# Four low parts, a row block of W_down, staging loads, two roots and a spread: moved or rewritten in a hybrid gMLP and Mamba-2 layer

## The chip, the core and the metric

The kernel runs on one core of a Trainium2 chip. TensorE multiplies matrices, VectorE (DVE), ScalarE (ACT) and GpSimd (POOL) work elementwise, and SyncE (SP) issues transfers. The metric is the device time of one launch in microseconds.

## What is computed

One layer on 1024 tokens of 1024 channels, everything in fp32:

```python
h   = RMSNorm_pre(x)
P   = h @ W_in                    # u, v (gMLP, 512 each), z (512), x, B, C (512, 256, 256), dt (8)
A   = u * (W_s layer_norm(gelu(v)) + b)          # within chunks of 128 tokens, causal
B   = rms(ssd(conv(x, B, C), dt) * silu(z))      # 8 heads of 64, 2 groups of 128 states
x   = x + RMSNorm_post(concat[A, B] @ W_out)
x   = x + RMSNorm_post2(relu(RMSNorm_pre2(x) @ W_up)^2 @ W_down)     # 4096 hidden
```

## The kernel before

A product in fp32 is made of three products of shorter numbers: each operand is split in a high part (a cast, names ending in h) and a low part (the number less its high part, names ending in l), and TensorE adds high by high, low by high and high by low. The splitting of the weights goes on beside the products all through the kernel. The high part is cast by ACT, and the low part is a subtraction, up to W_out on POOL and in W_down on VectorE.

The 1024 tokens are taken in two halves of 512. In a half the weights come in units of 512 KB: units 0 to 7 make B, C and x, 8 to 11 z, 12 to 15 v, 16 to 19 u, and 20 to 23 the first four blocks of W_out; the second half then uses the same units again. For each unit SP loads the weights into a staging buffer ws (there are two), ACT casts wh, the low part wl is subtracted from ws and wh, and where the unit comes again, `keep` stores wl to DRAM (wd). In the second half `again` loads ws once more for the cast and loads wl from wd. SP is one queue: a transfer that waits for its data or its buffer holds up those behind it.

The program's start is an order written by hand (PRO_OPS): for a token tile t, S sums squares on ACT, R makes the reciprocal root on VectorE (Newton steps on one column, each waiting for the last), N multiplies by the root and the norm weights wpre, T transposes on TensorE, H and L split the transposed tile hT. W and V are the cast and the low part of units 0 and 1, M and C a multiplication of tile 2 on POOL and ACT. PRO_LOADS is the order of the first loads: digits for token tiles, w for wpre, a and b for units 0 and 1. What follows, until the W_up products, is ordered by a scheduler that takes its estimates and the dependences; where an engine is `held`, it keeps the order in which the code is written. gg is the decay tile of the Mamba part, loaded by SP from the DRAM tile acd; carry is the last three columns of a block of x, B or C, kept for the convolution. The later token tiles are transposed into tx and split into hTh and hTl as the first.

The gate norm (second function below) makes a root for each token and spreads the four chunks' columns along 128 columns in the bank psgr, by a product with the identity.

W_down is a list `seq` of products, VectorE held. For product m the loop writes the load of piece m + 3, the splitting of piece m + 2 (`preps`), the products, and, at the last of a group, the emptying of the four PSUM banks into an accumulator (`flush`). The last four row blocks of W_down stand behind `seq` in the same lists; their low parts are wldl0 to wldl3, and their products go into the banks pl.

Of the kernel before, what the change touches and what calls it, by code (L numbers as in the profile page):

```python
# [13 lines left out]
ALU = mybir.AluOpType  # L14

P = 128
SEQ = 1024
D = 1024
# [28 lines left out]

PRO_LOADS = "0w1a23b"  # L50
PRO_BANK = (0, 0, 1, 2)
PRO_OPS = ("S0 R0 S1 W0 N0 R1 T0 H00 N1 V0 S2 H01 L00 S3 L01 T1 H10 L10 M2 H11 R23 W1 V1 L11 N3 C2 "
           "T2 T3 H20 H21 L21 H31 H30 L20 L30 L31 X")


# [1 line left out]
def hymba_kernel(ctx, tc, x, norm_mix_pre, w_in, gm_ln_w, gm_ln_b, gm_w_s, gm_b_s,  # L57
                 conv_w, conv_b, dt_bias, a_log, d_skip, ssm_norm_w, w_out,
                 norm_mix_post, norm_ffn_pre, w_up, w_down, norm_ffn_post, out):
    nc = tc.nc  # L60
# [51 lines left out]
    def f(ap):  # L112
        return ap.bitcast(F32)
# [93 lines left out]
    staged = {}  # L207
# [10 lines left out]
    def load_unit(eng=None):  # L218
        i = state["load"]
        if i >= len(units):  # L220
            return
        state["load"] += 1
        if id(units[i]) in first:
            again(i)
            return
        first[id(units[i])] = i
        if i not in staged:
            stage_unit(i)
        st, shape = staged.pop(i)
        wh = wpool.tile(shape, F32R, tag="wh", bufs=N_SPLIT, name=f"wh{i}")  # L230
        wl = wpool.tile(shape, F32R, tag="wl", bufs=N_SPLIT, name=f"wl{i}")
        split(wh, wl, st, eng)
        ready.append((wh, wl))
        keep(i)

    def keep(i):

# [4 lines left out]
    def again(i):  # L242
        if i not in staged:
            stage_unit(i)
        st, shape = staged.pop(i)
        wh, wl = [wpool.tile(shape, F32R, tag=t_, bufs=N_SPLIT, name=f"{t_}{i}") for t_ in ("wh", "wl")]
        nc.sync.dma_start(f(wl.rearrange("p a b -> p (a b)")), parts[first[id(units[i])]])
        act.copy(wh, st)
        ready.append((wh, wl))

# [116 lines left out]
    def step(op):  # L367
        kind, arg = op[0], op[1:]
        t = int(arg[0]) if arg else 0
        if kind == "S":  # L370
            ssx[t] = sumsq(x0[t], f"ssx0{t}")
        elif kind == "R":
            chains = [rstd_steps(ssx[int(c)], D) for c in arg]
            for c, steps in zip(arg, chains):
                rx[int(c)] = next(steps)
            while chains:
                chains = [c for c in chains if next(c, 0) is None]
        elif kind == "N":
            dve.scalar_tensor_tensor(x0[t], x0[t], rx[t], wpre, op0=ALU.mult, op1=ALU.mult)
        elif kind == "M":  # L380
            for q in range(2):
                qs = slice(q * 512, (q + 1) * 512)
                pool.tensor_tensor(x0[t][:, qs], x0[t][:, qs], wpre[:, qs], op=ALU.mult)
        elif kind == "C":
            act.activation(x0[t], x0[t], AF.Copy, scale=rx[t])
        elif kind == "T":
            for q in range(2):
                ps = (mm_bank, ss_bank, mi_bank)[PRO_BANK[t]](f"tx0{t}_{q}")
                psx[t, q] = ps.rearrange("p (k c) -> p k c", c=P)
                for k in range(4):  # L390
                    c0 = (4 * q + k) * P
                    pe.transpose(psx[t, q][:, k, :], x0[t][:, c0:c0 + P], ident)
        elif kind in "HL":
            q = int(arg[1])
            h, l = [y[:, 4 * q:4 * q + 4, t * P:(t + 1) * P] for y in hT]
            if kind == "H":
                act.copy(h, psx[t, q])
            else:
                dve.tensor_tensor(l, psx[t, q], f(h), op=ALU.subtract)
        elif kind == "W":  # L400
            st, shape = staged.pop(t)
            wh = wpool.tile(shape, F32R, tag="wh", bufs=N_SPLIT, name=f"wh{t}")
            wl = wpool.tile(shape, F32R, tag="wl", bufs=N_SPLIT, name=f"wl{t}")
            act.copy(wh, st)
            units01[t] = wh, wl, st
        elif kind == "V":
            wh, wl, st = units01[t]
            pool.tensor_tensor(wl, st, f(wh), op=ALU.subtract)
            ready.append((wh, wl))
            first[id(units[t])] = t  # L410
            keep(t)
            state["load"] += 1
        else:
            small_setup()
# [306 lines left out]
    def gate_norm(H, g):  # L721
        nm = f"{g}{H.tg}"
        if g == 0:
            H.mb = s8("mixbh" + H.tg, F32R), s8("mixbl" + H.tg, F32R)
        mh, ml = H.mb
        zs = H.zt[2 * g], H.zt[2 * g + 1]
        for i in range(2):
            y = H.xg[g][:, i, :]
            dve.tensor_mul(y, y, zs[i])
            act.activation(zs[i], y, AF.Square)  # L730
        dve.tensor_add(zs[0], zs[0], zs[1])
        ps = mi_bank("psgn" + nm)
        for c in range(NCH):
            pe.matmul(ps[:, c:c + 1], lhsT=zs[0][:, c * P:(c + 1) * P], rhs=ones[:, 0:1],
                      start=True, stop=True)
        rt = row_rstd(ps[:, 0:NCH], 256)
        r = mi_bank("psgr" + nm)
        for c in range(NCH):
            pe.matmul(r[:, c * P:(c + 1) * P], lhsT=rt[:, c:c + 1].broadcast_to([P, P]), rhs=ident,
                      start=True, stop=True)  # L740
        for i in range(2):
            b = 2 * g + i
            y = H.xg[g][:, i, :]
            dve.scalar_tensor_tensor(y, y, cols[:, 40 + b:41 + b], r, op0=ALU.mult, op1=ALU.mult)
            split(mh[:, b, :], ml[:, b, :], y)
            H.mix[4 + b] = (mh[:, b, :], ml[:, b, :])
# [484 lines left out]
    for m, (n, g, i) in enumerate(seq):  # L1231
        gs = SG[n]
        k = m - seq.index((n, gs[0], ORD[0]))
        if k == len(gs):
            w_load(n + 1, 0)
        elif k == 5 * len(gs) + 1:
            w_load(n + 1, 1)
        floads[m + 3]()
        preps[m + 2]()
        (fh, fl), (h, l) = pcs[g, i]  # L1240
        if g == gs[0]:
            banks[i] = banks[MORE[i]] if i in MORE else \
                psum2.tile([P, 4, 512], F32, tag=f"pd{(n + (i != 1)) % 2}", bufs=1, name=f"pd{n}_{i}")
        ps = banks[i]
        for t in range(4):
            tsl = slice(t * P, (t + 1) * P)
            for q in range(2):
                mm3(ps[:, t, :], fh[:, q, tsl], fl[:, q, tsl], h[:, q, :], l[:, q, :],
                    g == gs[0] and q == 0 and i not in MORE, g == gs[-1] and q == 1,
                    skip_group_check=i in MORE)  # L1250
        if g == gs[-1]:
            flush(i, ps)
    for m in range(len(seq) + 2, len(preps)):
        if m + 1 < len(preps):
            floads[m + 1]()
        preps[m]()
    wfpost = now["nwp"].tile([P, D], F32, name="wfpost")
    after_w(nc.sync.dma_start(wfpost, norm_ffn_post[0].partition_broadcast(P)))
    pctx2.close()
# [114 lines left out]
```

## Time and profile before

| | |
|---|---|
| median of three runs | 1056.06 us (1054.29 to 1058.64) |
| the profiled execution, whole | 1053.96 us |
| its span in the profile | 1052.2 us |
| TensorE busy | 1016.0 us, 97% |
| VectorE busy | 758.9 us, 72% |
| ACT busy | 492.4 us, 47% |
| POOL busy | 307.1 us, 29% |

A span is the time from the first to the last instruction. The busy shares are means over stages with different limits, so the rows below go by stretches and by single waits. In a timeline a row has its start, its duration, the engine, the line, the operation, its output and inputs, and in brackets the idle time ahead of it with what released it. All engine operations have line 73, that of a helper.

### The profile page before, as it was taken

What the parts mean: (1) busy time and instruction counts of PE and PEld (TensorE: products, weight loads), DVE (VectorE), ACT (ScalarE), POOL (GpSimd) and SP (SyncE); (2) the same over time, 40 slices, a digit from 0 to 9 for tenths busy, and PEclk for the clock granted to TensorE, in tenths of its full rate; (3) what the DMA queues carried; (4) which work ended last, traced back from release to release, by engine and by line L of the source; (5) the groups of instructions that cost most, each with busy time, mean ns of one, the idle gap of its engine ahead of it and who ended that gap; (6) DMA issues with size and microseconds to landing.
All of it is one profiled execution on the core that took longest, in us unless ns stands there. A gap on an engine that the chain in (4) does not pass through costs nothing.

```text
span 1052.2 us, 13180 instructions
## 1 busy us (share of the span) xinstructions
PE 1016.0 (97%) x4735; PEld 830.5 (79%) x4735; DVE 758.9 (72%) x1281; ACT 492.4 (47%) x668; POOL 307.1 (29%) x155
## 2 busy tenths in 40 slices
PE   4999998999999999999999999999999999999996
PEld 4877777777788888888888888888788888888875
DVE  5656978266964835666577777775678888879877
ACT  5537554354554533675444444444634324333421
POOL 4533333020001102400111111111653444535533
PEclk9999999999999999999999999999999999999998
DMA  7857635455984263766757777766852634534332
GB/s 248 254 166 236 197 124 190 146 172 184 371 284 136 97 230 121 231 191 195 264 187 233 235 225 236 226 228 213 294 173 99 228 117 138 180 101 145 136 140 100
DMA packets 147625, 201.77 MB, mean 192 GB/s; under 512 B 9204, under 2 KB 84072, under 8 KB 147560
## 3 DMA queue, kind: packets, MB, share of 16 engines
q1 hardware_dynamic: 113128, 182.06, 51.5%
q10 hardware_dynamic: 34432, 18.88, 6.2%
q8 instruction: 37, 0.61, 0.2%
q14 instruction: 28, 0.23, 0.1%
HBM read 143.73 MB, written 57.18 MB: 191 GB/s over the span
## 4 chain that ended last, share of the span: by engine, by line
PE 78%; DVE 11%; DMA 5%; ACT 3%; SPq 1%; issue 1%; POOL 0%; DVEq 0%; ACTq 0%
PE pd L73 25%; PE puC L73 8%; PE puB L73 8%; PE pe L73 8%; PE pso L73 7%; PE puD L73 4%; PE pl L73 4%; DMA gg<-acd 3%; PE psz L73 3%; PE psv L73 2%; PE psu L73 2%; PE psB L73 2%; PE psC L73 2%; DVE xg L73 1%; DVE v L73 1%
## 5 line engine op out<-in xcount | busy, mean ns | idle before, releaser
L73 PE MATMUL pd<-whd,f 128*128 128x512 f32 x752 | 232.0, 390 | 0.0
L73 PEld LDWEIGHTS pd<-whd,f 128*128 128x128 f32 x752 | 141.3, 188 | 29.3 <-issue 0.3
L73 POOL TENSOR_TENSOR f<-fr,f 128x1024 fp32r<-128x1024 f32 x47 | 119.2, 2539 | 135.2 <-ACT f L73 135.2
L73 PE MATMUL pd<-wld,f 128*128 128x512 f32 x376 | 146.5, 390 | 0.8 <-DVE wld L73 0.8
L73 POOL TENSOR_TENSOR wl<-ws,wh 128x1024 fp32r<-128x1024 f32 x36 | 88.6, 2466 | 186.8 <-ACT wh L73 180.7
L73 ACT CAST wh<-ws 128x1024 fp32r<-128x1024 f32 x72 | 75.2, 1046 | 74.6 <-PE pso L73 17.0
L73 POOL TENSOR_TENSOR wlb<-sa,whb 128x1024 fp32r<-128x1024 f32 x16 | 38.5, 2407 | 222.3 <-ACT whb L73 222.3
L73 PEld LDWEIGHTS pd<-wld,f 128*128 128x128 f32 x376 | 70.6, 188 | 15.9 <-DVE wld L73 1.2
L73 ACT CAST f<-fr 128x1024 fp32r<-128x1024 f32 x47 | 49.0, 1049 | 55.0 <-PE pd L73 35.1
L73 ACT CAST whd<-wt 128x1024 fp32r<-128x1024 f32 x28 | 29.5, 1052 | 93.9 <-DVE wt L73 93.4
L73 DVE TENSOR_TENSOR acc<-pd,acc 128x2048 f32<-128x2048 f32 x24 | 54.9, 2287 | 11.9 <-PE pd L73 8.8
L73 DVE TENSOR_TENSOR wld<-wt,whd 128x1024 fp32r<-128x1024 f32 x28 | 36.7, 1310 | 35.2 <-ACT whd L73 34.1
L73 ACT ACTIVATE u<-u 128x512 f32<-128x512 f32 (+1 forms) x66 | 44.3, 671 | 37.1 <-DVE u L73 31.4
L73 DVE TENSOR_TENSOR wld<-wr,whd 128x1024 fp32r<-128x1024 f32 x21 | 60.0, 2887 | 0.7 <-ACT whd L73 0.7
L73 PE MATMUL pe<-hTh,wh 128*128 128x512 f32 x128 | 50.3, 393 | 0.0
L73 DVE TENSOR_TENSOR u<-puB,s 128x512 f32<-128x512 f32 x32 | 22.1, 691 | 38.6 <-PE puB L73 24.0
L73 PE MATMUL pe<-hTl,wh 128*128 128x512 f32 x128 | 49.9, 390 | 0.0
L73 PE MATMUL pe<-hTh,wl 128*128 128x512 f32 x128 | 49.9, 390 | 0.0
L73 ACT ACT_TABLE_LOAD x28 | 35.9, 1283 | 24.5 <-DVE carry L73 4.9
L73 DVE TENSOR_TENSOR wt<-wr,wt 128x1024 f32<-128x1024 f32 x14 | 35.9, 2561 | 0.0
L73 ACT ACTIVATE f<-f 128x512 f32<-128x512 f32 x32 | 20.2, 632 | 32.2 <-DVE f L73 31.7
L73 POOL TENSOR_TENSOR dec<-st,cd 128x256 f32<-128x256 f32 x12 | 7.4, 614 | 89.7 <-DVE st L73 85.4
(343 smaller groups left out, 2680.6 us busy)
## 6 DMA issues: line engine op xcount, KB each, us to landing
fr<-fsp SPq DMA_DIRECT2D x49, 512.0 KB, 3.6
ws<-in_w_in_dram SPq DMA_DIRECT2D x40, 512.0 KB, 5.3
wu<-in_w_up_dram ACTq DMA_DIRECT2D x32, 512.0 KB, 4.0
wr<-in_w_down_dram SPq DMA_DIRECT2D x32, 512.0 KB, 4.9
wd<-wl SPq DMA_DIRECT2D x28, 512.0 KB, 3.5
wl<-wd SPq DMA_DIRECT2D x28, 512.0 KB, 5.4
fsp<-c SPq DMA_DIRECT2D x42, 256.0 KB, 2.0
ws<-in_w_out_dram SPq DMA_DIRECT2D x16, 512.0 KB, 3.8
```

The lines of the kernel that those rows point to most:

```text
L73: ins = fn(*a, **k)
```

## The change

Seven edits. The load of token tile 1 goes ahead of that of wpre. In the hand-written order the roots of tiles 0 and 1 become one step (Q): six steps of the first, then the rest of it and the second's interleaved; both multiplies come behind it, S2 and S3 stand between the H copies, and unit 0's low part is on VectorE. The low parts of units 20 to 23 are on VectorE too. A unit's code now writes the next unit's staging load ahead of the store of its own low part, and in the second half ahead of the load of its own low part, which is put behind the next staging load in the order. The spread into psgr is made by a transpose. At the last product of W_down's list, the third last row block is split ahead of the emptying.

```diff
@@ -47,9 +47,9 @@
 
 
 
-PRO_LOADS = "0w1a23b"
+PRO_LOADS = "01wa23b"
 PRO_BANK = (0, 0, 1, 2)
-PRO_OPS = ("S0 R0 S1 W0 N0 R1 T0 H00 N1 V0 S2 H01 L00 S3 L01 T1 H10 L10 M2 H11 R23 W1 V1 L11 N3 C2 "
+PRO_OPS = ("S0 S1 Q01 W0 N0 T0 N1 H00 L00 V0 H01 L01 T1 S2 H10 L10 S3 H11 L11 M2 R23 W1 V1 N3 C2 "
            "T2 T3 H20 H21 L21 H31 H30 L20 L30 L31 X")
 
 
@@ -229,9 +229,14 @@
         st, shape = staged.pop(i)
         wh = wpool.tile(shape, F32R, tag="wh", bufs=N_SPLIT, name=f"wh{i}")
         wl = wpool.tile(shape, F32R, tag="wl", bufs=N_SPLIT, name=f"wl{i}")
-        split(wh, wl, st, eng)
+        split(wh, wl, st, dve if any(units[i] is u for u in wou[0:4]) else eng)
         ready.append((wh, wl))
+        stage_next(i)
         keep(i)
+
+    def stage_next(i):
+        if i + 1 < len(units) and i + 1 not in staged:
+            stage_unit(i + 1)
 
     def keep(i):
 
@@ -244,7 +249,10 @@
             stage_unit(i)
         st, shape = staged.pop(i)
         wh, wl = [wpool.tile(shape, F32R, tag=t_, bufs=N_SPLIT, name=f"{t_}{i}") for t_ in ("wh", "wl")]
-        nc.sync.dma_start(f(wl.rearrange("p a b -> p (a b)")), parts[first[id(units[i])]])
+        stage_next(i)
+        low = nc.sync.dma_start(f(wl.rearrange("p a b -> p (a b)")), parts[first[id(units[i])]])
+        if i + 1 < len(units):
+            after(low, i + 1)
         act.copy(wh, st)
         ready.append((wh, wl))
 
@@ -373,6 +381,14 @@
             chains = [rstd_steps(ssx[int(c)], D) for c in arg]
             for c, steps in zip(arg, chains):
                 rx[int(c)] = next(steps)
+            while chains:
+                chains = [c for c in chains if next(c, 0) is None]
+        elif kind == "Q":
+            a, b = [rstd_steps(ssx[int(c)], D) for c in arg]
+            rx[int(arg[0])], rx[int(arg[1])] = next(a), next(b)
+            for _ in range(6):
+                next(a)
+            chains = [a, b]
             while chains:
                 chains = [c for c in chains if next(c, 0) is None]
         elif kind == "N":
@@ -405,7 +421,7 @@
             units01[t] = wh, wl, st
         elif kind == "V":
             wh, wl, st = units01[t]
-            pool.tensor_tensor(wl, st, f(wh), op=ALU.subtract)
+            (pool if t else dve).tensor_tensor(wl, st, f(wh), op=ALU.subtract)
             ready.append((wh, wl))
             first[id(units[t])] = t
             keep(t)
@@ -736,8 +752,7 @@
         rt = row_rstd(ps[:, 0:NCH], 256)
         r = mi_bank("psgr" + nm)
         for c in range(NCH):
-            pe.matmul(r[:, c * P:(c + 1) * P], lhsT=rt[:, c:c + 1].broadcast_to([P, P]), rhs=ident,
-                      start=True, stop=True)
+            pe.transpose(r[:, c * P:(c + 1) * P], rt[:, c:c + 1].broadcast_to([P, P]), ident)
         for i in range(2):
             b = 2 * g + i
             y = H.xg[g][:, i, :]
@@ -1236,7 +1251,11 @@
         elif k == 5 * len(gs) + 1:
             w_load(n + 1, 1)
         floads[m + 3]()
+        if m == len(seq) - 1:
+            floads[m + 4]()
         preps[m + 2]()
+        if m == len(seq) - 1:
+            preps[m + 3]()
         (fh, fl), (h, l) = pcs[g, i]
         if g == gs[0]:
             banks[i] = banks[MORE[i]] if i in MORE else \
@@ -1250,10 +1269,7 @@
                     skip_group_check=i in MORE)
         if g == gs[-1]:
             flush(i, ps)
-    for m in range(len(seq) + 2, len(preps)):
-        if m + 1 < len(preps):
-            floads[m + 1]()
-        preps[m]()
+    preps[-1]()
     wfpost = now["nwp"].tile([P, D], F32, name="wfpost")
     after_w(nc.sync.dma_start(wfpost, norm_ffn_post[0].partition_broadcast(P)))
     pctx2.close()
```

ACT between the casts of units 10 and 12 (wh10 to wh12), in the kernel before. gg00 and gg01 are the decay tiles of the first chunk, xg0 and xg1 the convolved x of the two groups:

```order
L73 CAST wh10_1060<-ws10_1058 128x1024
L73 ACTIVATE gg00_0_599<-gg00_0_599 128x512
L73 ACTIVATE gg01_0_621<-gg01_0_621 128x512
L73 CAST wh11_1095<-ws11_1093 128x1024
L73 ACTIVATE xg1_0_842<-psx2_0_817,cols_118 128x512
L73 ACT_TABLE_LOAD
L73 ACTIVATE xg1_0_842<-xg1_0_842 128x512
L73 CAST wh12_1130<-ws12_1128 128x1024
```

The same place now:

```order
L73 CAST wh10_1060<-ws10_855 128x1024
L73 CAST wh11_1095<-ws11_1064 128x1024
L73 ACTIVATE xg1_0_844<-psx2_0_819,cols_118 128x512
L73 ACTIVATE gg00_0_601<-gg00_0_601 128x512
L73 ACTIVATE gg01_0_623<-gg01_0_623 128x512
L73 CAST wh12_1130<-ws12_1099 128x1024
```

The cast of unit 11 and the first convolution step (xg from psx) have moved ahead of the two exponentials.

VectorE ahead of W_out in the first half, in the kernel before: the normalised v, the small root rr6 of the gate norm, and the low parts hTl of the token tiles 11 and 12:

```order
L73 TENSOR_TENSOR hTl_106<-tx11_0_1610,hTh_105 128x4x128
L73 TENSOR_TENSOR v_0_1274<-v_0_1274,lnw_888 128x512
L73 TENSOR_TENSOR hTl_106<-tx11_1_1617,hTh_105 128x4x128
L73 TENSOR_TENSOR v_0_1274<-v_0_1274,lnw_888 128x512
L73 TENSOR_SCALAR rti6_1250<-rv6_1247 128x4
L73 TENSOR_TENSOR v_0_1274<-v_0_1274,lnb_889 128x512 x4
L73 TENSOR_SCALAR rr6_1248<-rti6_1250 128x4
L73 TENSOR_TENSOR rt6_1249<-rv6_1247,rr6_1248 128x4
L73 TENSOR_TENSOR rt6_1249<-rt6_1249,rr6_1248 128x4
L73 SCALAR_TENSOR_TENSOR rr6_1248<-rt6_1249,rr6_1248 128x4
L73 TENSOR_TENSOR rt6_1249<-rv6_1247,rr6_1248 128x4
L73 TENSOR_TENSOR hTl_106<-tx12_0_1669,hTh_105 128x4x128
```

The same place now, in two pieces; first from the same first row to the low part of unit 22:

```order
L73 TENSOR_TENSOR hTl_106<-tx11_0_1612,hTh_105 128x4x128
L73 TENSOR_TENSOR v_0_1276<-v_0_1276,lnb_891 128x512 x2
L73 TENSOR_TENSOR wl21_1792<-ws21_1787,wh21_1791 128x1024
L73 TENSOR_TENSOR v_0_1276<-v_0_1276,lnb_891 128x512
L73 TENSOR_SCALAR rti6_1252<-rv6_1249 128x4
L73 TENSOR_TENSOR v_0_1276<-v_0_1276,lnb_891 128x512
L73 TENSOR_TENSOR wl22_1800<-ws22_1795,wh22_1799 128x1024
```

And around that of unit 23:

```order
L73 SCALAR_TENSOR_TENSOR rr6_1250<-rt6_1251,rr6_1250 128x4
L73 TENSOR_TENSOR rt6_1251<-rv6_1249,rr6_1250 128x4
L73 TENSOR_TENSOR wl23_1832<-ws23_1803,wh23_1831 128x1024
L73 TENSOR_TENSOR rt6_1251<-rt6_1251,rr6_1250 128x4
L73 TENSOR_TENSOR hTl_106<-tx12_1_1678,hTh_105 128x4x128
L73 SCALAR_TENSOR_TENSOR rr6_1250<-rt6_1251,rr6_1250 128x4
L73 TENSOR_TENSOR hTl_106<-tx13_0_1705,hTh_105 128x4x128
```

Three subtractions (wl21, wl22, wl23) have come in, the last of them between steps of the root rr6 and ahead of the hTl of the second half of tile 12 (tx12_1).

VectorE at the end of W_down, in the kernel before (acc21 is the emptying):

```order
L73 TENSOR_TENSOR wldl0_8283<-wr8_7917,whdl0_8282 128x1024
L73 TENSOR_TENSOR wldl1_8317<-wr9_8241,whdl1_8316 128x1024
L73 TENSOR_TENSOR acc21_6528<-pd3_1_7855,acc21_6528 128x2048
L73 TENSOR_TENSOR wldl2_8352<-wr8_7917,whdl2_8351 128x1024
L73 TENSOR_TENSOR wldl3_8360<-wr9_8241,whdl3_8359 128x1024
```

The same place now:

```order
L73 TENSOR_TENSOR wldl0_8283<-wr8_7917,whdl0_8282 128x1024
L73 TENSOR_TENSOR wldl1_8319<-wr9_8241,whdl1_8318 128x1024
L73 TENSOR_TENSOR wldl2_8327<-wr8_7917,whdl2_8326 128x1024
L73 TENSOR_TENSOR acc21_6528<-pd3_1_7855,acc21_6528 128x2048
L73 TENSOR_TENSOR wldl3_8360<-wr9_8241,whdl3_8359 128x1024
```

The low part wldl2 has moved ahead of the emptying.

## Rows read from the trace of the kernel before

**Rows 1.** The page's busy times: engine, busy us, share of the span, instructions.

```profile
PE 1016.0 (97%) x4735; PEld 830.5 (79%) x4735; DVE 758.9 (72%) x1281; ACT 492.4 (47%) x668; POOL 307.1 (29%) x155
```

**Rows 2.** Waits of TensorE: for whom, us in total, times, longest.

```profile
PE tx L73 <- DVE rv L73: 9.1, 1, 9.1
...
PE tx L73 <- DVE hTl L73: 2.4, 1, 2.4
...
PE psx L73 <- ACT wh L73: 1.3, 1, 1.3
...
PE pl L73 <- DVE acc L73: 0.8, 1, 0.8
...
PE psC L73 <- DVE gg L73: 0.6, 1, 0.6
```

**Rows 3.** Stretches: length, busy by engine (instructions), granted clock, DMA share, GB/s.

```profile
core 0: us, PE busy (x) PEld busy (x) DVE busy (x) ACT busy (x) POOL busy (x), PEclk, DMA share, GB/s
...
60.00:100.00 40.00, 37.90 (x197) 29.48 (x196) 22.64 (x64) 21.53 (x27) 14.28 (x9) 1.00 0.65 202
...
140.00:180.00 40.00, 37.33 (x188) 30.77 (x187) 33.45 (x70) 20.88 (x28) 10.91 (x6) 0.96 0.48 160
...
745.00:950.00 205.00, 205.00 (x905) 169.63 (x905) 170.37 (x80) 82.03 (x81) 98.02 (x39) 1.00 0.46 157
```

**Rows 4.** The same view, the two microseconds behind the wait for hTl.

```profile
176.00:178.00 2.00, 2.00 (x11) 1.86 (x10) 1.46 (x3) 1.47 (x2) 0.00 (x0) 0.50 0.93 302
```

**Rows 5.** Timeline of the start, ACT, VectorE and POOL.

```profile
7.67 1.28 DVE L73 SCALAR_TENSOR_TENSOR x<-x,rr,wpre 128x1024 f32<-128x1024 f32 x1
7.67 1.06 ACT L73 ACTIVATE ssx01j<-x 128x1024 bf16<-128x1024 f32 x1 [2.28 <-DMA x<-in_x_dram]
...
10.30 2.35 POOL L73 TENSOR_TENSOR wl<-ws,wh 128x1024 fp32r<-128x1024 f32 x1 [8.53 <-ACT wh L73]
...
11.10 2.63 DVE L73 SCALAR_TENSOR_TENSOR x<-x,rr,wpre 128x1024 f32<-128x1024 f32 x1
```

**Rows 6.** Timeline from 66 to 84, one row each of ACT, POOL, SP and TensorE.

```profile
72.36 1.03 ACT L73 CAST wh<-ws 128x1024 fp32r<-128x1024 f32 x1
...
73.47 2.39 POOL L73 TENSOR_TENSOR wl<-ws,wh 128x1024 fp32r<-128x1024 f32 x1 [8.63 <-ACT wh L73]
...
76.79 0.70 SPq L607 DMA_DIRECT2D gg<-acd  x1
...
76.63 0.47 PE L73 MATMUL psz<-hTh,wh 128*128 128x512 f32 x1 [0.67 <-DVE carry L73]
```

**Rows 7.** Timeline from 140 to 178, VectorE and then POOL.

```profile
145.75 2.46 DVE L73 TENSOR_REDUCE mu<-v 128x8 f32<-128x512 f32 x4 [4.19 <-ACT v L73]
...
162.22 1.29 DVE L73 TENSOR_TENSOR v<-v,lnw 128x512 f32<-128x512 f32 x2
...
164.02 2.49 DVE L73 TENSOR_TENSOR v<-v,lnw 128x512 f32<-128x512 f32 x1
...
167.03 2.29 DVE L73 TENSOR_TENSOR v<-v,lnw 128x512 f32<-128x512 f32 x1
...
171.92 0.17 DVE L73 TENSOR_TENSOR rt<-rv,rr 128x4 f32<-128x4 f32 x1
172.12 2.21 DVE L73 TENSOR_TENSOR rt<-rt,rr 128x4 f32<-128x4 f32 x1
...
163.56 5.22 POOL L73 TENSOR_TENSOR wl<-ws,wh 128x1024 fp32r<-128x1024 f32 x2 [18.59 <-ACT wh L73]
171.94 2.38 POOL L73 TENSOR_TENSOR wl<-ws,wh 128x1024 fp32r<-128x1024 f32 x1 [3.16 <-DMA wd<-wl]
```

**Rows 8.** The page's group of VectorE's low parts in W_down: busy, mean ns.

```profile
L73 DVE TENSOR_TENSOR wld<-wt,whd 128x1024 fp32r<-128x1024 f32 x28 | 36.7, 1310 | 35.2 <-ACT whd L73 34.1
```

**Rows 9.** Timeline of the tail, VectorE and then POOL.

```profile
992.23 5.37 DVE L73 TENSOR_TENSOR wldl<-wr,whdl 128x1024 fp32r<-128x1024 f32 x2
998.40 2.29 DVE L73 TENSOR_TENSOR acc<-pd,acc 128x2048 f32<-128x2048 f32 x1 [0.80 <-PE pd L73]
...
993.91 2.61 POOL L73 TENSOR_TENSOR f1l<-frl,f0l 128x1024 fp32r<-128x1024 f32 x1 [0.73 <-ACT f0l L73]
```

## The prediction

> **What bounds the kernel now.** I read the page's busy times first, then the waits of TensorE, then its busy time in stretches, and last the timelines around the few waits. TensorE is busy for 1016.0 of 1052.2 us [rows 1], so the change can win only what TensorE idles, and the end of the program behind its last matmul. Its waits name the places [rows 2]: 9.1 us before the first transpose, 1.3 us for the cast of unit 2, 2.4 us for a low part hTl in the middle, 0.6 us for a gg, 0.8 us for a bank in the tail. By stretches [rows 3] 2.10 us are idle in 60 to 100 and 2.67 in 140 to 180; between 745 and 950, as in most of what lies behind 340, TensorE never stops, and no edit touches its work there. After the 2.4 us wait the clock falls as well: 11 matmuls took all of 176 to 178 at a granted clock of 0.50, the 1.2 GHz level [rows 4]. Some 1 us goes with that, half of the stretch.
>
> **The start (staging loads, joined roots, unit 0's low part on VectorE).** ACT waits 2.28 us for tile 1, whose load is issued behind the norm weights [rows 5]. It now goes ahead of them, so tile 1's sum of squares starts up to 2.28 us earlier. Tile 0 pays: its multiply now comes behind the root of tile 1 too, which took 2.15 us, the time from the end of the one multiply (8.95) to the start of the other (11.10) [rows 5]. So tile 0's transposes come up to 2.2 us later and tile 1's up to 2.28 us earlier. I book neither: the first block of products needs both tiles, and the copies H10 and H11 that it waits for now stand behind the sums S2 and S3 on ACT, so I leave its start where it is. The multiply of tile 1 took 2.63 us, with POOL's low part (2.35 us from 10.30) beside it; that of tile 0, alone, 1.28 [rows 5]. With the low part on VectorE 1.35 us come back, and the low part itself costs 1.31 us there [rows 8]: an exchange. What can be won is in the order of TensorE. Eleven more matmuls of 256 columns now stand ahead of the wait for unit 2's cast, which is 1.3 us long [rows 2]. 905 matmuls, nearly all of 512 columns, took 205.00 us [rows 3], 0.227 each, so one of 256 is worth 0.113 and the eleven 1.25. With the wait itself as the bound that is 1.3 us at best. Against it, the load of unit 2 stands on SP behind the store of unit 0's low part, which POOL ended at 12.65 [rows 5]. On VectorE the low part stands behind both multiplies and one hTl; by the rows above it ends between 13 and 15, and I count up to 1 us of that for the cast. I take a gain of **0.3 us**, from -1.0 to +1.3.
>
> **The staging loads in 60 to 140.** SP issues in order. The load of the decay tile gg went out at 76.79, behind the store of unit 11's low part, and that behind POOL's subtraction (73.47) and ACT's cast, which ran only at 72.36, behind two exponentials [rows 6]. In the new order of ACT that cast and the first convolution step stand ahead of the exponentials. So the 0.67 us wait for the carry at 76.63 [rows 6], which is fed by that step, should go, and gg can be issued some 3 us earlier. But the wait for gg is 0.6 us only [rows 2], and the later gg of the second group is put behind one more store and load; its consumers stand 10 to 26 matmuls (2.3 to 5.9 us at 0.227 each) later on TensorE, which about covers it. I take a gain of **1.0 us**, from a loss of 1.0 to the 2.10 us that are idle in 60 to 100 [rows 3].
>
> **The low parts of W_out on VectorE.** Four subtractions leave POOL, 2.38 to 2.61 us each [rows 7], for VectorE at 1.31 us (the same shape there [rows 8]). The first lands in VectorE's 4.19 us of waiting for ACT before 145.75 [rows 7]: nothing. The other three lie on the chain that ends in the hTl for which TensorE waits: 3 x 1.31 = +3.93 us. Against it stands what POOL costs VectorE now. While POOL ran the units 21 and 22 (163.56, 5.22 us) and 23 (171.94, 2.38 us), multiplies with lnw took 2.49 and 2.29 us where two others took 1.29 together, and a tiny product of 4 columns took 2.21 us where its neighbour took 0.17 [rows 7]. That is 1.84 + 1.64 + 2.04 = 5.52 us, all on the same chain. So the chain gets 5.52 - 3.93 = 1.6 us shorter if all of it returns. This is the trace's reading; the Trainium skill agrees (SBUF — State Buffer, "Who interferes with whom"): a VectorE instruction with two SBUF inputs and a GpSimd instruction that reads SBUF exclude each other, whichever starts first holding the ports to its end. By that rule alone the edit would win the whole 1.6 us.
> I book less, since the order moves too: the third low part now stands between the steps of the last root, ahead of the hTl of tile 12's second half, and TensorE needs that half before all of tile 13's transposes; it needs a load (unit 23) that goes out behind one more store. I expect TensorE's wait there to end about 0.5 us earlier, **0.5 us** of gain; from 2.67 (all idle of the stretch) to a loss of 3.93 + 0.5 for the load.
>
> **The second half's loads.** A staging load goes ahead of the low part's load in every unit. The order of SP alternated so in most places before; TensorE's waits there are single ones under 1 us. I take nothing, plus or minus 1.0. The transposes into psgr replace as many matmuls of the same 128 columns, 8 in each half; 11 instructions of about this size took 2.00 us at half the clock, 0.18 each [rows 4], and since only the form differs I book nothing.
>
> **The tail.** Two low parts of the last row blocks end at 997.6, the emptying starts at 998.40 when TensorE has filled its banks, and TensorE waits 0.8 us for it [rows 2, 9]. A third low part in between takes 1.31 us, since POOL is done at 996.5 [rows 9]: the emptying starts 0.5 us later, but TensorE has three more matmuls (0.68 us) to do before it. **0.2 us** of gain; 0.8 at best, a loss of 0.9 if POOL's work moves on top of it and the third takes 2.6 us.
>
> **Sum.** 0.3 + 1.0 + 0.5 + 0.0 + 0.2 = 2.0 us. The profiled execution took 1053.96, 1.8 more than its span, and is 2.1 below the median of the runs. So 1051.96 of its kind, or 1054.06 as a median: **1054.1**.
>
> **Rivals.** (a) *More comes back.* If VectorE's locks go and nothing new is late, the 2.4 us wait and its slow clock go wholly: 2.44 + 1.0; with 1.3 from the start and 1.6 from 60 to 140 that is 6.3 us, 1049.8. For it: 5.52 us of locks against 3.93 of new work; the rule of the Trainium skill named above (SBUF — State Buffer, "Who interferes with whom") would return all of the 5.52. Against: TensorE's order there changes with it. (b) *VectorE becomes the bound before W_out.* In the new order the product of z and the hTl of tile 10 stand between the first two steps of the large root and wait there for ACT. If that waiting eats the returned 5.52 us, the three low parts make the chain 3.93 us longer and unit 23's load 0.5; TensorE idles longer and runs another 1 us of transposes at the 1.2 GHz level: +5.4, 1061.5. It decides once the hTl of tile 12's second half ends later than about 176, when TensorE asks for it. (c) *The order does nothing*: TensorE's queue hides each shift as it hides them now, 0 +- 1: 1056.
>
> **Chances.** The forecast 0.47, (a) 0.22, (b) 0.13, (c) 0.18. A measurement of this kernel can tell about 0.5%, 5.3 us. Faster than 1050.8: most of (a) and little of the forecast, 0.20. Slower than 1061.3: half of (b) and a little of the unpriced, 0.08. Within: 0.72. The range goes from 1049.6, the lower end of (a), to 1059.6, the sum with the losses of start and W_out together (1.0 + 4.4), which leaves out (b)'s worse half.
>
> **What would show it.** Right, if the wait for the carry at 76.6 is gone; if no multiply on VectorE between 157 and 178 takes over 1 us but for the 1.31 us low parts; if the 1.3 us wait before unit 2's first matmul is shorter; if 0.50 of the clock at 176 to 178 is shorter. Wrong, if TensorE waits longer than 2.4 us between 170 and 180, if unit 2's cast comes after 20.5, if new waits stand in 100 to 140 for gg, or if the emptying in the tail starts after 999.5. It would also be wrong if the second half, 196 to 420, gained or lost more than 1 us, of which nothing in the rows speaks.

## The result and the profile after

The changed kernel takes 1046.73 us (median of four runs, 1045.17 to 1048.03) against 1055.26 us: the ratio is 0.9911, with a 95% interval from 0.9883 to 0.994, some 9 us less. In two later sets of runs, beside experiments, its ratio to the kernel before was 0.9932 (0.9917 to 0.9947) and 0.9948 (0.9931 to 0.9965). So by the three ratios the change is worth 5.5 to 9.4 us, where 2.0 had been forecast, and the first median lies 2.9 us below the range.

The page's busy times, span first, for the changed kernel (beside [rows 1]):

```profile
span 1046.3 us, 13148 instructions
## 1 busy us (share of the span) xinstructions
PE 1013.2 (97%) x4719; PEld 828.5 (79%) x4719; DVE 755.8 (72%) x1286; ACT 493.3 (47%) x668; POOL 292.7 (28%) x150
```

The span is 5.9 us shorter. TensorE is busy 2.8 us less and runs 16 matmuls fewer; the other 3.1 us are idle time. These are single executions: in the two later profiles of the changed kernel (e5 and e13 below) the spans are 1046.5 and 1051.3 us, and TensorE is busy for 1015.2 and 1015.0. The waits of TensorE in the changed kernel, for whom, total, times, longest (beside [rows 2]):

```profile
PE tx L73 <- DVE x L73: 11.1, 1, 11.1
PE psx L73 <- ACT wh L73: 2.3, 1, 2.3
PE psz L73 <- DVE carry L73: 2.3, 1, 2.3
PE tx L73 <- DVE hTl L73: 1.9, 1, 1.9
...
PE pl L73 <- DVE acc L73: 0.4, 1, 0.4
```

Two waits grew (unit 2's cast, the carry), two shrank (hTl, the tail's bank), and that for gg is gone. The stretches that gained are seen in the windows, the changed kernel first, then the one row of the kernel before that was not shown (length, busy by engine with instructions, granted clock, DMA share, GB/s):

```profile
60.00:100.00 40.00, 37.69 (x186) 30.03 (x185) 25.77 (x63) 22.13 (x30) 14.77 (x9) 0.96 0.61 198
100.00:140.00 40.00, 40.00 (x216) 32.19 (x215) 32.34 (x103) 24.41 (x33) 17.23 (x10) 1.00 0.68 228
140.00:180.00 40.00, 37.37 (x192) 30.54 (x191) 34.87 (x81) 21.41 (x29) 2.54 (x2) 1.00 0.40 131
```

```profile
100.00:140.00 40.00, 37.67 (x198) 29.84 (x197) 37.00 (x106) 22.93 (x31) 16.20 (x10) 1.00 0.59 193
```

Between 100 and 140 TensorE idled 2.33 us before and not at all now. In 60 to 100 nothing was won ([rows 3] has 37.90), and the clock fell there. The starts of the first matmul into some tiles, read from the timelines, show where these two executions part. The last column is the best kernel of the experiments:

| first matmul into | before | changed | difference | units 12, 15 too (e16) |
|---|---|---|---|---|
| psx, 1st half | 20.25 | 21.59 | +1.34 | 21.47 |
| psz, 1st half | 76.63 | 78.48 | +1.85 | 75.03 |
| psv, 1st half | 106.57 | 108.11 | +1.54 | 103.00 |
| pso, 1st half | 166.31 | 164.54 | -1.77 | 159.34 |
| psd, 2nd half | 199.31 | 195.55 | -3.76 | 188.80 |
| pe (W_up) | 418.94 | 413.06 | -5.88 | 406.19 |
| pl (tail) | 998.20 | 992.73 | -5.47 | 987.67 |

One execution is not all of a kernel, though. In the eight profiles whose start has the old code, the first psx came anywhere from 20.24 to 20.95, and psr, near 30 us, from 29.6 to 31.8. The wait at 285.56 of the kernel before (0.85 us, behind another of 0.84) is missing in e10's profile, which has the same code there. The changed kernel's own three profiles reach pe at 413.06, 413.32 and 415.84 and pl at 992.73, 992.93 and 997.73, while e10, which differs from the kernel before in the tail alone, reaches pe at 415.43. So the last rows of the table are no price of the change; the price is in the ratios. From psd to pe the code of the kernel before took 219.63 us in its own profile and 217.24 in e10's, and the changed kernel 217.51, 218.26 and 219.11: no gain can be read there.

### The profile page after: what moved, and what is told of

Its sections match the earlier page's. It is cut to its first block, busy times and chain, and to the rows that moved or that the text cites. A ratio compares the mean times of both kernels' runs of the same rounds, so it can differ in the third digit from the quotient of the medians.

```text
span 1046.3 us, 13148 instructions
## 1 busy us (share of the span) xinstructions
PE 1013.2 (97%) x4719; PEld 828.5 (79%) x4719; DVE 755.8 (72%) x1286; ACT 493.3 (47%) x668; POOL 292.7 (28%) x150
## 4 chain that ended last, share of the span: by engine, by line
PE 82%; DVE 9%; DMA 4%; ACT 3%; issue 1%; POOL 0%; DVEq 0%; ACTq 0%; SPq 0%; POOLq 0%
PE pd L73 23%; PE puC L73 8%; PE puB L73 8%; PE pso L73 8%; PE pe L73 6%; PE psz L73 4%; PE puD L73 4%; PE psv L73 4%; PE pl L73 4%; PE psC L73 3%; PE psB L73 3%; PE psu L73 2%; DMA gg<-acd 2%; PE psx L73 1%; DVE xg L73 1%
## 5 line engine op out<-in xcount | busy, mean ns | idle before, releaser
L73 POOL TENSOR_TENSOR wl<-ws,wh 128x1024 fp32r<-128x1024 f32 x31 | 75.0, 2425 | 151.4 <-ACT wh L73 145.1
L73 ACT CAST whd<-wt 128x1024 fp32r<-128x1024 f32 x28 | 29.5, 1052 | 93.8 <-DVE wt L73 93.3
L73 ACT ACTIVATE f<-f 128x512 f32<-128x512 f32 x32 | 20.2, 632 | 32.1 <-DVE f L73 31.6
L73 POOL TENSOR_TENSOR mixbl<-xg,mixbh 128x512 fp32r<-128x512 f32 x8 | 10.6, 1352 | 88.1 <-ACT mixbh L73 88.1
```

Source lines behind the costliest of these rows:

```text
L73: ins = fn(*a, **k)
```

## The experiments

Each kernel was timed beside the kernel before on one chip; e1 to e4 on one, e5 to e8 on another, e9 to e12 and e13 to e16 on two more. The ratio is to the kernel before. Two views stood against each other: that the edits work through the order that the scheduler finds once they are there, and the prediction's, in which each edit has its own price. In each expectation, A and B are the two theories of that run.

### One edit at a time

**e1, the start alone.**

```diff
-PRO_LOADS = "0w1a23b"
+PRO_LOADS = "01wa23b"
-PRO_OPS = ("S0 R0 S1 W0 N0 R1 T0 H00 N1 V0 S2 H01 L00 S3 L01 T1 H10 L10 M2 H11 R23 W1 V1 L11 N3 C2 "
+PRO_OPS = ("S0 S1 Q01 W0 N0 T0 N1 H00 L00 V0 H01 L01 T1 S2 H10 L10 S3 H11 L11 M2 R23 W1 V1 N3 C2 "
+        elif kind == "Q":
...
-            pool.tensor_tensor(wl, st, f(wh), op=ALU.subtract)
+            (pool if t else dve).tensor_tensor(wl, st, f(wh), op=ALU.subtract)
```

> The kernel before with the start alone changed: the first loads, the joined roots, the order of the first copies and sums, unit 0's low part on VectorE. Its instruction order on every engine shows that this edit by itself already moves ACT's cast of unit 11 ahead of the exponentials and the psC, psA and psB products of the Mamba part 10 to 26 places later on TensorE. Theory A (the gain in 100 to 140 is made by the start's edit through the order that the scheduler then finds): TensorE's small waits in 100 to 140 (2.3 us of idle time before) are gone, 1.4 us are lost by 30, some 2 to 3 us more are lost around 78, together -0.5 us (range -3 to +1) against the kernel before. Theory B (the prediction's: the staging loads of each unit do it): the waits in 100 to 140 stay, and the start gives 0.3 us.

Measured: 1052.77 against 1053.63, ratio 0.9995 (0.9981 to 1.0009). Its windows:

```profile
60.00:100.00 40.00, 37.69 (x186) 30.00 (x185) 25.18 (x66) 22.18 (x28) 13.77 (x8) 0.96 0.65 208
100.00:140.00 40.00, 39.23 (x213) 31.35 (x212) 32.58 (x102) 23.92 (x33) 17.66 (x10) 1.00 0.63 214
140.00:180.00 40.00, 36.75 (x184) 30.43 (x183) 34.09 (x72) 20.87 (x29) 11.97 (x6) 0.96 0.43 145
```

The start alone makes TensorE 1.56 us busier in 100 to 140, and it makes the wait of 2.3 us for the carry. Theory A has the place right, and its -0.5 us for the whole, though B's 0.3 lies in the interval too. The 1.4 us lost by 30 did not show: psr, the matmul that starts near 30, came at 29.30 here and at 31.01 in the changed kernel. What differed is the granted clock: in 22 to 24 it was 0.50, the 1.2 GHz level, in the changed kernel and 1.00 here. Of all 18 profiles the seven with 0.50 there, of either start, have psr at 30.4 to 31.8, the others at 28.4 to 30.3.

**e2, the spread alone.**

```diff
-            pe.matmul(r[:, c * P:(c + 1) * P], lhsT=rt[:, c:c + 1].broadcast_to([P, P]), rhs=ident,
-                      start=True, stop=True)
+            pe.transpose(r[:, c * P:(c + 1) * P], rt[:, c:c + 1].broadcast_to([P, P]), ident)
```

> The kernel before with the spread into psgr by a transpose alone. Theory A: each matmul of the spread is two passes on TensorE and a transpose one; TensorE runs 16 instructions fewer of 0.112 us, 1.8 us less busy time and 1.8 us less of the whole. Theory B (the prediction's): same shape, same time, 0 us.

Measured: 1050.85, ratio 0.9975 (0.9965 to 0.9985), 2.6 us less (1.6 to 3.7). The instructions into psgr, first in the kernel before and then here (count, duration in ns, first and last start):

```profile
L73 PEld LDWEIGHTS psgr<-ident,rr x32: 187/191/334, 123.9 to 360.1; 128*128 128x128 f32 x32
L73 PE MATMUL psgr<-ident,rr x32: 272/276/527, 124.0 to 360.2; 128*128 128x128 f32 x32
```

```profile
L73 PEld LDWEIGHTS psgr<-ident,rr x16: 134/137/139, 125.4 to 358.1; 128*128 128x128 f32 x16
L73 PE MATMUL psgr<-ident,rr x16: 271/273/273, 125.6 to 358.2; 128*128 128x128 f32 x16
```

Each of the 16 written matmuls ran as two, each transpose as one, and a matmul instruction lasts as long in either (272 and 271 ns). Back to back they start some 0.112 us apart, so 16 x 0.112 = 1.8 us of TensorE's time are gone (its busy time here is 1014.1 us, 1.9 less). Theory B, the prediction's, falls. The 0.8 us beyond that lie within the interval.

**e3, the low parts of units 20 to 23 alone.**

```diff
-        split(wh, wl, st, eng)
+        split(wh, wl, st, dve if any(units[i] is u for u in wou[0:4]) else eng)
```

> The kernel before with the low parts of units 20 to 23 on VectorE alone. Theory A: the multiplies and the small root's steps between 157 and 178 run unlocked, TensorE's wait for hTl at 175 gets shorter by 1 to 1.6 us and its stretch at the 1.2 GHz level with it: 1.4 us less in all. Theory B (rival of the prediction): VectorE becomes the bound, the wait grows to over 3 us: 1 to 5 us slower.

Measured: 1055.35, ratio 1.0017 (1.0007 to 1.0028): 1.8 us slower. The wait for hTl is gone, and another stands a little further on; VectorE's and TensorE's timeline at this place:

```profile
171.73 0.16 DVE L73 TENSOR_TENSOR rt<-rt,rr 128x4 f32<-128x4 f32 x1
172.58 1.23 DVE L73 TENSOR_TENSOR wl<-ws,wh 128x1024 fp32r<-128x1024 f32 x1 [0.68 <-DMA wd<-wl]
173.72 0.15 DVE L73 SCALAR_TENSOR_TENSOR rr<-rt,rr 128x4 f32<-128x4 f32 x1
173.79 1.28 DVE L73 TENSOR_TENSOR hTl<-tx,hTh 128x512 fp32r<-128x512 f32 x2
...
175.37 0.16 DVE L73 SCALAR_TENSOR_TENSOR rr<-rt,rr 128x4 f32<-128x4 f32 x1
```

```profile
175.59 1.16 PE L73 MATMUL psgr<-ident,rr 128*128 128x128 f32 x8 [2.65 <-DVE rr L73]
```

The locks went as foretold (no multiply takes over 0.7 us, each low part 1.21 to 1.23). But unit 23's low part, which waits 0.68 us for the store of an earlier low part (wd), stands between the steps of the small root, and so do two hTl; the spread waits for the root's last step. That this wait makes the 1.8 us is not shown: it replaces one of 2.44 us (2.57 in e10 and e4), and from the first pso to psd e3 takes as long as the kernel before (table below).

**e4, the second half's loads alone.**

```diff
-        nc.sync.dma_start(f(wl.rearrange("p a b -> p (a b)")), parts[first[id(units[i])]])
+        stage_next(i)
+        low = nc.sync.dma_start(f(wl.rearrange("p a b -> p (a b)")), parts[first[id(units[i])]])
+        if i + 1 < len(units):
+            after(low, i + 1)
```

> The kernel before with the second half's loads alone changed (the next staging load ahead of the low part's load, the low part's load behind it). Theory A: TensorE's waits at 284.05 and 285.56 (1.7 us) shrink to one of 0.5: 1.2 us less. Theory B (the prediction's): nothing, within 1 us; what changed at 280 in the changed kernel comes from elsewhere.

Measured: 1053.38, ratio 1.0001 (0.9988 to 1.0014). Nothing, as the prediction had it.

**e10, the tail alone** (the hunks on `floads[m + 4]`, `preps[m + 3]` and `preps[-1]`).

> The kernel before with the tail alone changed. The prediction: TensorE's 0.8 us wait at 1000.7 shrinks, 0.2 us faster in all; the trace of the changed kernel says 0.3 to 0.45. Rival: POOL's work moves onto the third low part, 0.9 us slower.

Measured: 1053.71 against 1053.55, ratio 1.0005 (0.9986 to 1.0024). The wait in the tail went from 0.80 to 0.37 us, and 0.4 us is too little to be seen in the whole.

The seventh edit, the staging load ahead of the store of the own low part, was not run: with that line and without it, in either kernel, the order of the instructions on all engines is the same.

The single edits thus add up to -0.5 - 2.6 + 1.8 + 0.1 + 0.5 = -0.7 us, each with an interval of 1 to 2 us to either side, where the whole gives -5.5 to -9.4. They are not independent.

### One edit taken back

**e5, the changed kernel; e6, without the start; e7, without the spread; e8, without the low parts on VectorE.** The edits are those of e1, e2 and e3 reversed.

> The changed kernel again, beside the next three on one chip. If the four single edits simply add up (start -0.9, spread -2.6, low parts of W_out +1.8, loads of the second half 0), it is 1 to 2.5 us faster than the kernel before; if they need each other, 7 to 9 us, as in its first runs.

> The changed kernel with the start of the kernel before. Theory A (the start's edit orders 60 to 180 and the other edits need that order): the small waits in 100 to 140 come back, the wait ahead of psgr at 175 grows, 4 to 6 us slower than the changed kernel. Theory B (edits add up): 0.5 us slower.

> The changed kernel with the spread as a product again. Both theories: 16 instructions more on TensorE, 1.8 us. Theory A adds that the scheduler's order at 160 to 180 falls back (psgr again ahead of the second half of tile 13): 2 to 4 us slower than the changed kernel. Theory B: 2.6 us slower.

> The changed kernel with the low parts of units 20 to 23 on POOL again. Theory A: POOL's subtractions lock VectorE's multiplies again and the wait at 173 grows from 1.9 to about 3 us: 1 to 2 us slower than the changed kernel. Theory B (the single run was 1.8 us slower with them on VectorE): 1.8 us faster than the changed kernel.

| | median | ratio to the kernel before |
|---|---|---|
| e5, changed | 1048.32 | 0.9932 (0.9917 to 0.9947) |
| e6, no start | 1046.73 | 0.9925 (0.9909 to 0.9942) |
| e7, no spread | 1051.40 | 0.9964 (0.9946 to 0.9983) |
| e8, no low parts | 1048.76 | 0.9948 (0.9929 to 0.9967) |

By the ratios the spread is worth 3.4 us here, with 2.5 to either side, which does not tell the 2 to 4 of its theory A from the 2.6 of B. The low parts are worth 1.7, also with 2.5 to either side, so that they gain anything in this company is not shown, where alone they cost 1.8 with 1.1 to either side. Without them (e8) the multiplies are locked again and TensorE waits 2.9 us for rr ahead of psgr, as its theory A had it. The start is worth nothing: theory A of e6 was wrong in that the other edits do not need its order.

### Which edits need each other

**e9, spread and low parts on the kernel before; e15, those and the second half's loads.**

> The kernel before with two edits together: the spread by a transpose, and the low parts of units 20 to 23 on VectorE. Theory A (the two need each other: with the transpose the scheduler puts all steps of the small root ahead of unit 23's low part on VectorE, where with the low parts alone the last three steps came behind it and behind two hTl): the wait of 2.65 us ahead of psgr in the single run is gone or under 1.3 us; 4 to 7 us faster than the kernel before. Theory B (they add up, -2.6 and +1.8): 0.8 us faster.

> Three edits on the kernel before: the spread by a transpose, the low parts of units 20 to 23 on VectorE, the second half's loads. The start and the tail are those of the kernel before. Theory A (the gain is made by these three): 6 to 8 us faster than the kernel before, within 1 us of the changed kernel. Theory B (the start's order is needed for it): 3 us slower than the changed kernel.

e9: 1048.90, ratio 0.995 (0.9934 to 0.9966), 5.3 us less where the single edits add to 0.8. e15: 1048.64, ratio 0.9946 (0.9931 to 0.9961); the changed kernel on the same chip (e13) 1048.47, ratio 0.9948. In time, two edits make what can be measured of the whole, and more than their sum. The place is the one of the wait in e3; VectorE's timeline in e9:

```profile
170.84 0.16 DVE L73 TENSOR_TENSOR rt<-rt,rr 128x4 f32<-128x4 f32 x1
171.04 0.16 DVE L73 SCALAR_TENSOR_TENSOR rr<-rt,rr 128x4 f32<-128x4 f32 x1
172.25 1.23 DVE L73 TENSOR_TENSOR wl<-ws,wh 128x1024 fp32r<-128x1024 f32 x1 [1.05 <-DMA wd<-wl]
173.39 1.40 DVE L73 SCALAR_TENSOR_TENSOR xg<-xg,cols,psgr 128x512 f32<-128x512 f32 x2
174.71 1.28 DVE L73 TENSOR_TENSOR hTl<-tx,hTh 128x512 fp32r<-128x512 f32 x2
```

With the transpose the order puts the root's last step ahead of unit 23's low part; it ends at 171.2 instead of 175.5, and no wait stands ahead of psgr. What is left is 1.3 us for the product behind it (pssp, waiting for xg).

The profiles bear this place out. The columns are the start of the first pso, the time from there to the second half's first psd, and TensorE's idle time in it:

| start, and which of the two edits | first pso | to psd | idle |
|---|---|---|---|
| old, none (before, e4, e10) | 165.98 to 166.46 | 32.2 to 33.0 | 3.5 to 3.9 |
| old, spread (e2) | 167.04 | 31.9 | 4.1 |
| old, low parts (e3) | 165.43 | 32.3 | 4.1 |
| old, both (e6, e9, e15) | 164.84 to 166.73 | 29.5 to 31.6 | 2.0 to 2.4 |
| new, none (e1) | 163.92 | 34.1 | 3.8 |
| new, spread (e8) | 162.41 | 33.1 | 3.7 |
| new, low parts (e7) | 162.50 | 32.6 | 3.8 |
| new, both (changed, e5, e11, e13, e14) | 162.84 to 164.54 | 31.0 to 32.4 | 2.8 to 4.1 |

With the old start neither edit alone takes idle time away here, and the two together take 1.1 to 1.8 us. The changed kernel does not win in this way: unit 23's low part stands between the steps of its root (at 171.54, with the last step at 173.35), and the wait for hTl is there. Its new start has the first pso some 2 us earlier than e6, e9 and e15, and that is given back by psd (194.7 to 196.7, where those three have 195.2 to 196.5). So e9 and the changed kernel come to the same time by two ways; why the new start's order keeps the root apart, no run separates.

**e11 and e14, the changed kernel without the second half's loads; e13, the changed kernel beside e14.**

> The changed kernel with the second half's loads of the kernel before. If that edit is worth nothing (as alone, ratio 1.0001), the same as the changed kernel within 1 us. If the changed kernel's shorter waits at 280 come from it, 1.3 us slower.

> The changed kernel beside the next three on one chip, as their yardstick: ratio 0.991 to 0.994 to the kernel before, as in its two earlier sets.

> The changed kernel with the second half's loads of the kernel before, now beside the changed kernel. Theory A (that edit is worth something beside the others, whose profile shows the waits at 280 to 286 at 0.5 us with it and 1.5 without): 1 to 1.5 us slower than the changed kernel. Theory B (nothing, as alone): the same within 0.7 us.

e11: 1049.22, ratio 0.9949 (0.9929 to 0.9969). e14: 1047.42, ratio 0.9939 (0.9918 to 0.996), against e13's 0.9948, which itself lies a little outside the 0.991 to 0.994 expected of it. Theory B of e14 holds: the loads of the second half are worth nothing that can be measured, with the others or without.

### The wait that the start brought

In the changed kernel TensorE waits 2.31 us for the carry. VectorE's and POOL's timeline ahead of it:

```profile
73.61 0.68 DVE L73 TENSOR_TENSOR gg<-gg,cbm 128x512 f32<-128x512 f32 x1
74.21 0.74 DVE L73 SCALAR_TENSOR_TENSOR xg<-psx,cols,xg 128x510 f32<-128x510 f32 x1
74.87 2.74 DVE L73 TENSOR_TENSOR gg<-gg,cbm 128x512 f32<-128x512 f32 x1
77.53 0.74 DVE L73 SCALAR_TENSOR_TENSOR xg<-psx,cols,xg 128x511 f32<-128x511 f32 x1
78.19 0.15 DVE L73 COPY carry<-psx 128x3 f32<-128x3 f32 x1
```

```profile
74.71 2.34 POOL L73 TENSOR_TENSOR wl<-ws,wh 128x1024 fp32r<-128x1024 f32 x1 [3.14 <-ACT wh L73]
```

The second gg product took 2.74 us where the first took 0.68, with POOL's low part of unit 12 beside it, and the carry stands behind.

**e12, unit 12's low part on VectorE too; e16, those of units 12 and 15.**

```diff
-        split(wh, wl, st, dve if any(units[i] is u for u in wou[0:4]) else eng)
+        split(wh, wl, st, dve if i in (12, 15) or any(units[i] is u for u in wou[0:4]) else eng)
```

> The changed kernel with one more low part, that of unit 12, on VectorE. In the changed kernel POOL's low part of unit 12 (74.71, 2.34 us) runs beside VectorE's gg product, which takes 2.74 us for 0.68, and the carry for which TensorE waits 2.31 us comes behind it. On VectorE the low part stands behind the carry. Theory A (port locks are what places the waits): TensorE's wait there falls under 0.5 us, its products at the 1.2 GHz level behind it (8 of 0.43 us for 0.23) go too, 2 to 4 us faster than the changed kernel. Theory B: what is late is the gg's load, the wait stays, and the 1.31 us come on top: 0 to 1.3 us slower.

> The changed kernel with the low parts of units 12 and 15 on VectorE too. With unit 12's alone the wait at 78 was gone and given back at 125, where POOL's low part of unit 15 held a small step of the root rr5 for 2.33 us. If locks are what places these waits, neither of the two waits is there and the gain arrives at the end, less what the wait at 173 takes back: 1 to 4 us faster than the changed kernel. If VectorE's chain ahead of W_out sets the time anyway, the gain is given back there: the same within 1 us.

e12: 1048.74, ratio 0.9945 (0.9929 to 0.9961): no faster than the changed kernel. The wait at 78 is gone (first psz at 74.86 instead of 77 to 78.5), but all of it is given back: of theory A the place came true and the 2 to 4 us did not. TensorE's waits in e12, and the step that made the third, with POOL's work beside it:

```profile
PE tx L73 <- DVE x L73: 10.6, 1, 10.6
PE tx L73 <- DVE hTl L73: 3.2, 1, 3.2
PE psgr L73 <- DVE rr L73: 1.7, 1, 1.7
```

```profile
119.73 2.33 DVE L73 TENSOR_SCALAR rr<-rti 128x4 int32<-128x4 int32 x1
```

```profile
119.67 2.37 POOL L73 TENSOR_TENSOR wl<-ws,wh 128x1024 fp32r<-128x1024 f32 x1
```

A step of four columns (0.16 us elsewhere) took 2.33 us while POOL made unit 15's low part. With that one moved too, e16 takes 1041.95, ratio 0.9878 (0.9859 to 0.9897): 6.5 us less than the changed kernel on the same chip (1048.47), more than the 1 to 4 expected, and the best of all. Its windows and waits:

```profile
60.00:100.00 40.00, 39.75 (x209) 31.70 (x208) 26.88 (x74) 24.33 (x30) 11.43 (x7) 1.00 0.72 230
100.00:140.00 40.00, 40.00 (x209) 32.45 (x208) 36.25 (x103) 22.55 (x31) 15.23 (x9) 1.00 0.67 218
140.00:180.00 40.00, 38.24 (x198) 31.25 (x198) 32.44 (x77) 20.09 (x29) 2.53 (x2) 1.00 0.45 145
```

```profile
PE tx L73 <- DVE x L73: 10.7, 1, 10.7
PE pso L73 <- ACT mixah L73: 1.5, 2, 0.7
PE pe L73 <- ACT e L73: 1.4, 1, 1.4
PE pso L73 <- ACT cd L73: 1.3, 1, 1.3
PE psx L73 <- ACT wh L73: 1.1, 1, 1.1
PE pssp L73 <- DVE xg L73: 0.9, 1, 0.9
```

The carry is waited for 0.2 us, rr and hTl not at all, and the granted clock stays at 1.00 from 10 to 420, where each of the changed kernel's three profiles has two or three falls to 0.50. That the lock on the small step alone made e12's loss is not shown apart: unit 15's low part alone was not moved, and with it the scheduler's order changed as well (the second half of tile 13 is now transposed behind the spread).

## Why the prediction was wrong

**The spread.** This is the step that failed worst, and the rows would have told it. "Since only the form differs I book nothing": the trace of the kernel before has 32 matmuls into psgr, where the code writes 16, and I took the two for the same count. The term measured 1.8 us of TensorE's time, 2.6 us of the whole alone, 3.4 beside the others (2.5 to either side). With 2.6 in its place the forecast would have been 1051.5, inside the range; the rest of the miss lies in the adding up (below).

**The staging loads in 60 to 140.** The section gave the new order to the wrong edit. The start's edit makes it (e1), the staging line moves nothing: e6, which has that line without the start, shows the old picture, 0.7 us of waiting for the carry and 1.66 us idle in 100 to 140. Of its contents: the cast of unit 11 did go ahead of the exponentials, but the wait for the carry did not go, it grew from 0.67 to 2.31 us, since POOL's next low part now fell on a gg product. The waits in 100 to 140, 2.33 us, all went; these the text had not priced, though it said that the consumers stand later. The term of 1.0 us measured nothing: what the new order wins ahead of the first pso it gives back by psd (table above), and e1 as a whole is the start's 0.3 us within its interval.

**The low parts of W_out.** The price of the lock was right: no multiply of v in the changed kernel takes over 0.7 us from 157 to 178. Of the 0.5 us for the wait about 0.3 came: it was 2.44 us before (2.57 in e10 and e4), and 1.91, 2.05 and 2.29 in the three profiles of the changed kernel (2.06 and 2.65 in e11 and e14, with the same code there). The 1 us for the clock behind it [rows 4] hung on one execution. The rows of e10, which has the same code there and waited longer, of the changed kernel, and of e5, the changed kernel again:

```profile
176.00:178.00 2.00, 1.97 (x14) 1.82 (x15) 1.95 (x4) 1.40 (x2) 0.00 (x0) 1.00 0.97 294
```

```profile
174.00:176.00 2.00, 1.45 (x10) 0.99 (x8) 1.48 (x3) 1.43 (x3) 0.00 (x0) 1.00 0.95 260
176.00:178.00 2.00, 1.82 (x8) 1.62 (x9) 1.90 (x6) 1.13 (x3) 1.31 (x2) 1.00 1.08 331
```

```profile
174.00:176.00 2.00, 1.99 (x5) 1.12 (x5) 2.00 (x4) 1.47 (x3) 0.97 (x1) 0.50 1.07 323
```

Rival (a) comes nearest in number (1049.8) and not in the way: it has that 1.0 us in it, and its wait did not go. Rival (b) has the direction of the edit alone (e3 is slower), by a third of its 5.4 us, and not by its way, since the steps of the large root follow each other in e3 without a gap; the place that showed up, unit 23's low part among the steps of the small root, is the one that the forecast named for its caution. The mistake was to price the edit against the other edits' absence. Alone it costs 1.8 us, and with the spread it gains 2.6 (e9 against e2, on two chips, 2.0 to either side).

**The start.** Right in size (0.3 forecast; 0.5 with 1.5 to either side in e1, nothing in e6). The steps: ACT's wait for tile 1 fell from 2.28 to 0.16 us; the two multiplies together took 2.47 us, and the low part 1.22 us, ending at 14.6; unit 2's load went out at 15.10, 0.64 us later, inside the 1 us allowed. Unit 2's cast began at 20.49 (20.40 in e5, 19.95 in e13), at the edge of the 20.5 that was to be a sign of error. The 1.3 us wait for unit 2's cast, expected shorter, was 2.3 in this run and 0.6 to 2.6 in the nine other profiles that have the new start.

**The second half and the tail.** Right for the loads: 0 in e4 and e14. In the tail the wait went from 0.80 to 0.37 us; the emptying began at 993.19, as the third of the low parts ahead of it ended. The 0.2 us themselves are too small for e10 to show.

**The adding up, and the range.** The sum took the edits as independent, and this step failed too: the five single results add to -0.7 and the whole gives -5.5 to -9.4; two of them, -0.8 by their sum, give -5.3 together, 4.5 us more with 2.3 to either side. Edits that a scheduler answers with another order have to be priced together. The range was made of single prices and their ends. Its upper end was also added up wrong: losses of 1.0 and 4.4 in place of gains of 0.3 and 0.5 put 6.2 us on the forecast, 1060.3 and not 1059.6; the measurement lies at the other end, where 1049.6 is rival (a)'s time less 0.2 us that nothing accounts for.

## What to carry to other kernels

Count an instruction in the trace, not in the code, before an exchange is booked at nothing. Where a scheduler orders the program, compare the orders for each edit alone before its effect is given to it, and try edits together that meet on one engine. Before a microsecond in one profile is put down to an edit, look for it in a second profile of the same code. When a low part on POOL falls beside work with two inputs on VectorE, follow what stands behind it: here, when one lock was taken away the next one showed (e12), and the gain came with the second (e16).

## What the runs showed of the hardware

A fp32 matmul against the identity ran as two instructions and a transpose of the same 128 columns as one, some 0.112 us each. A VectorE step of four columns (TENSOR_SCALAR) was held for 2.33 us by a POOL subtraction that had started 0.06 us before; the same step took 2.33 us beside POOL's subtraction in e4 and e10 too. It has one tensor input, so the reading of the prediction, two SBUF inputs, is too narrow; the Trainium skill (SBUF — State Buffer, "Who interferes with whom") counts tensor_scalar among the forms that can contend when their operands meet certain conditions, and this row agrees. A step of one column was not held: in the kernel before, this one ran beside the POOL subtraction that started at 10.30 [rows 5]:

```profile
10.85 0.21 DVE L73 TENSOR_SCALAR rr<-rt,rr 128x1 f32<-128x1 f32 x1
```

The granted clock fell to 0.50, the 1.2 GHz level, behind the 2.3 us wait for the carry in seven of the eight profiles that have it, and stayed at 1.00 in e14. Behind the wait for hTl it fell after 2.44 us (the kernel before) and 2.05 (e5), and not after 2.57 (e10) or 1.91. So the length of the wait alone did not decide it.
